# Running the decay levels of both head pairs side by side, and four low parts of weights on GpSimd

## The chip, the cores and the metric

The kernel runs on one core of a Trainium2 chip, in one launch. The metric is the device time in microseconds (us); lower is better. The kernel before takes 292.37 us (median of three runs, 292.06 to 292.63). The engines are named as in the profile: PE (TensorE, matrix products), PEld (its weight loads), DVE (VectorE), ACT (ScalarE), POOL (GpSimd) and SP (SyncE, which issues the DMAs).

## The reference

One decoder layer over 512 tokens of width 1024. The input is normalised, and one projection makes eight groups of 512 columns from it. Four of them feed a gated recurrence of four heads (state 128x128, evaluated chunkwise), four feed block-sparse attention of eight heads (width 64). Both results are gated, joined and projected back.

```python
h = _rms_norm(x, norm_w[l])
proj = jnp.einsum("btd,dc->btc", h, w_in[l])
hq, hf, hi, hg, aq, ak, av, ag = jnp.split(proj, split_points, axis=-1)
o_h = _rms_norm(_hgrn2(hq, hf, hi, lower_bounds[l]), hg_norm_w[l]).reshape(B, T, HG_WIDTH)
o_h = o_h * jax.nn.silu(hg.astype(jnp.float32))
o_a = _moba(aq, ak, av, q_norm_w[l], k_norm_w[l]) * jax.nn.silu(ag.astype(jnp.float32))
x = x + jnp.einsum("btc,cd->btd", jnp.concatenate([o_h, o_a], axis=-1), w_out[l])
```

In the recurrence, with forget gate f, key k = 1 - f and value i, the state follows S_t = diag(f_t) S_{t-1} + k_t i_t^T, and the readout is o_t = S_t^T q_t.

## The kernel before

**Projection.** Operands are split into a high and a low part, and each product is made of three matrix products: high by high, low by high and high by low. Weights arrive in 40 pieces of 256 rows by 512 columns (`load`, lines 90 to 103). `split_hi` casts a piece to its high part `whi` on ACT (line 109); `split_lo` subtracts it to get the low part `wlo` (line 117), on GpSimd if the piece's number is in `POOL_LO`, else on DVE, and then issues the load of the piece three further on. A group takes four pieces, 4g to 4g+3. It is computed in four units of 128 rows; a unit is 24 products of 128x512, in trace and order `acc<-...`. The last unit of a group frees its pieces one by one and splits the piece six further on. Group 1 makes the gate f and the key k, group 2 the recurrence's q, group 3 its output gate G, group 4 the attention's gate gT, groups 5, 6 and 7 the attention's K, Q and v.

**Levels.** The decay inside a chunk of 128 tokens is handled by `levels(pr)` (lines 332 to 446), a generator for one pair of heads. It waits until f, k and q of its pair are there. POOL multiplies neighbouring gates together into products over 2, 4, ... 128 tokens (line 365). Then come five steps. In each PE multiplies blocks of k by blocks of q into a PSUM tile `pl`: 32 products of 32x64 in each of the first three steps, 16 of 32x32 in the fourth, 8 of 64x64 in the fifth. Each product is two instructions in the trace. DVE merges the result (line 351) or ACT copies it into the matrix `AT` (lines 415, 430, 443), and DVE scales q and k by the gate products for the next step (line 357).

**States, chunks, readouts.** When both pairs are through, `states()` turns k (`tp<-ident,k`), copies it to SBUF on ACT (line 458), multiplies it by the values (`us`) and builds the next state S on DVE (lines 466, 471), three times. `chunks()` computes the output of a chunk (`ops`: 4 products for chunk 0, 8 for each later one, since these also read S). `readout()` squares it on ACT (line 496), reduces it on DVE (line 498), raises it to the power -0.5 on POOL (line 163), scales it on DVE (line 505) and turns it on PE (`tp<-ident,scr`); ACT and DVE split the result into `mThh` and `mThl` (lines 516, 517).

**Order.** PE's order is fixed while the program is written, by a planner with a clock of its own. Every generator yields a latency from the table `LAT` and names of things it waits for; `drive` (line 203) steps a generator once its latency has passed on that clock, and fills in projection products (`fill_a`, line 817) as long as none is ready. At one place the filler itself stops. When the first unit of group 5 has been computed, `ev_qk` must reuse the buffers of f and k, and calls `wait_for("chunks")`:

```python
    def wait_for(*keys):
        while not all(kk in done for kk in keys):
            advance()
```

`advance` (line 198) moves the planner's clock to the next ready generator and steps it, with no filler in between. Orders of DVE, ACT and POOL are made by the tile framework; each engine runs its instructions strictly in its order.

Of the kernel before, what the change touches and what calls it, by code (L numbers as in the profile page):

```python
# [21 lines left out]
def kernel(  # L22
# [90 lines left out]
    def split_lo(n):  # L113
        raw = W.pop(("raw", n))
        hi, lo = W[n]
        eng = nc.gpsimd if n in POOL_LO else nc.vector
        eng.tensor_sub(lo, raw, hi.bitcast(F32))  # L117
# [3 lines left out]
    def split(n):  # L121
        if n < len(stream):
            split_hi(n)
            split_lo(n)

    POOL_LO = (3,)
    LAT = dict(lm=4.544, lev0=9.2567, lev=4.4882, copy=1.9908, rms=5.7036, silu=15.1764, qk=14.2881, soft=2.5598, softn=0.0041, acopy=4.5215, st=1.5748, ch=6.6909, DEPTH=2)
    SEQ = 'y10 nt t00 wh0 y1 t01 l00 y2 p00 wl0 p10 l01 t10 q00 t11 q10 l10 wh1 p30 q30 l11 wl1 p20 q20 t03 sq0 t12 t02 sq1 p01 q01 wh2 l03 l12 sq3 wh3 p21 q21 p11 q11 sq2 l02 p31 q31 wl2 p32 q32 rs wl3 p02 q02 p22 q22 cv t13 p12 q12 rr cm l13'
    DSEQ = 'x00 nw x10 w0 x20 x30 x01 x31 x11 w1 x21 w2 w4 v w3 w5'
    POOL_LO = (3,)  # L130
    for w in DSEQ.split():
        if w == "nw":
            nc.sync.dma_start(out=vec[32:40, :], in_=norm_w.rearrange("o (k p) -> (o k) p", p=P))  # L133
# [38 lines left out]
    def mm(o, a, b, start, stop, us):  # L172
        nc.tensor.matmul(o, a, b, start=start, stop=stop)  # L173
        clock[0] += us
# [5 lines left out]
    def spawn(gen, lat=0.0):  # L180
        threads.append([clock[0] + lat, (), gen, lat])
# [88 lines left out]
    def acc_tile(wide):  # L270
        return (psc if wide else pacc).tile([P, 512], F32, tag="sc" if wide else "acc", name="acc")
# [29 lines left out]
    def ev_i(u, ps):  # L301
        nc.scalar.activation(it[:, u, :], ps, AF.Copy, scale=rst[:, u:u + 1])
# [29 lines left out]
    def levels(pr):  # L332
# [4 lines left out]
        kk, qq = k[:, hs, :], q[:, hs, :]  # L337

        def blocks32(qs, w):
            pl = psc.tile([P, 512], F32, tag="sc", name="pl")  # L340
            plv = pl[:, 0:256 * w].rearrange("p (m w c) -> p m w c", w=w, c=32)
            for m in range(8):
                hd, n = divmod(m, 4)
                for b in range(4):
                    t0 = n * P + b * 32
                    mm(plv[b * 32:b * 32 + 32, m], kk[:, hd, t0:t0 + 32], qs[:, :, hd, t0:t0 + 32],
                       True, True, 0.035 if w == 1 else 0.047)
            return plv
# [7 lines left out]
        def mul(o, a, b):  # L356
            nc.vector.tensor_tensor(o, a, b, op=ALU.mult)
# [21 lines left out]
        def up_k(l):  # L379
            v, shape = halves(kk, l)  # L380
            mul(v[:, :, 0, :], v[:, :, 0, :], TB[l][:, :, 1:2].to_broadcast(shape))

        yield LAT["lev0"]
        plv = blocks32(q2[:, :, hs, :], 2)
# [7 lines left out]
        for l in (2, 4):  # L392
# [7 lines left out]
            mul(p0[:, :, 3, :], p0[:, :, 1, :], T4[:, :, 1:2].to_broadcast(one))  # L400
            yield LAT["lm"]
            plv = blocks32(q2[:, :, hs, :], 2)
# [13 lines left out]

        yield LAT["lev"]
        pl = psc.tile([P, 512], F32, tag="sc", name="pl")
        plv = pl[:, 0:128].rearrange("p (m c) -> p m c", c=32)
        atv = at.rearrange("p (m o) t -> p m o t", o=2)  # L420
        for m in range(8):
            hd, n = divmod(m, 4)
# [10 lines left out]

        yield LAT["lev"]
        pl = psc.tile([P, 512], F32, tag="sc", name="pl")
        plv = pl[:, 0:256].rearrange("p (m c) -> p m c", c=64)
        for m in range(8):
            hd, n = divmod(m, 4)
# [5 lines left out]
        up_q(7)  # L444
        up_k(7)
        done[("lev", pr)] = clock[0]

    S = [None] * NT

    def states():  # L450
        yield (LAT["st"], ("lev", 0), ("lev", 1))
        for n in range(NT - 1):
            cs = slice(n * P, (n + 1) * P)
            tp = ptr.tile([P, 512], F32, tag="tr", name="tp")
            for h in range(HH):
                tr(tp[:, h * P:(h + 1) * P], k[:, h, cs])
            kst = scratch()
            nc.scalar.copy(kst, tp)
            yield LAT["copy"]
            us = psc.tile([P, 512], F32, tag="sc", name="us")  # L460
            for h in range(HH):
                es = slice(h * DK, (h + 1) * DK)
                mm(us[:, es], kst[:, h * P:(h + 1) * P], it[:, n, es], True, True, 0.218)
            Sn = scratch()
            if n == 0:
                nc.vector.tensor_copy(Sn, us)
            else:
                for h in range(HH):
                    es = slice(h * DK, (h + 1) * DK)
                    m = (h % 2) * 4 + n  # L470
                    nc.vector.scalar_tensor_tensor(Sn[:, es], S[n][:, es], TL[h // 2][:, m:m + 1], us[:, es],
                                                   op0=ALU.mult, op1=ALU.add)
            S[n + 1] = Sn
            done[("S", n + 1)] = clock[0]

    def chunks():
        yield (LAT["st"], ("lev", 0), ("lev", 1))
        for n in range(NT):
            cs = slice(n * P, (n + 1) * P)
            ops = psc.tile([P, 512], F32, tag="sc", name="ops")  # L480
            for h in range(HH):
                es = slice(h * DK, (h + 1) * DK)
                mm(ops[:, es], AT[h // 2][:, (h % 2) * 4 + n, :], it[:, n, es], True, n == 0, 0.218)
                if n > 0:
                    mm(ops[:, es], q[:, h, cs], S[n][:, es], False, True, 0.218)
            spawn(readout(n, ops), LAT["rms"])
            if n < NT - 1:
                yield (LAT["ch"], ("S", n + 1))
        done["chunks"] = clock[0]
# [97 lines left out]
    DEPTH = LAT.get("DEPTH", 2)  # L587
# [77 lines left out]
    def start_attention():  # L665
        for p in range(NP):
            c_ = {}
            for m, tiles in enumerate(UNITS):
                spawn(attn_unit(p * len(UNITS) + m, p, tiles, c_))
# [147 lines left out]
    def fill_a():  # L817
        const_tri()
        yield from group(1, True, ev_f)
        yield from group(2, True, ev_silu_t(q2[:, 0]))  # L820
        yield from group(3, False, ev_silu(G))
        yield from group(4, True, ev_silu_t(gT))
        const_dist()
        yield from group(5, False, ev_qk("K", ("f", "k", "i", "KL"), kgs))
        yield from group(6, False, ev_qk("Q", ("q",), qgs))
        yield from group(7, False, ev_v)

    with tc.manual_schedule(engines={mybir.EngineType.PE}):
        with tc.manual_schedule():
            accs = {}  # L830

            def part(u, kp, low):
                us = slice(u * P, (u + 1) * P)
                if u not in accs:
                    accs[u] = acc_tile(u >= 2)
                hi, lo = W[kp]
                for d in range(2):
                    kt = 2 * kp + d
                    wh, wl = hi[:, d, :], lo[:, d, :]
                    prods = ((hTh[:, kt, us], wl),) if low else ((hTh[:, kt, us], wh), (hTl[:, kt, us], wh))  # L840
                    for j, (a, b) in enumerate(prods):
                        mm(accs[u], a, b, kt == 0 and not low and j == 0, kt == KT - 1 and low, 0.216)

            def part_hi(u, kp):
                part(u, kp, False)

            def part_lo(u, kp):
                part(u, kp, True)

            acts = dict(cm=const_masks, cv=const_vec, sq=x_sq, rs=x_rstd, rr=x_rows, y=warm_up, nt=nw_col, t=x_turn, l=x_lo, p=part_hi, q=part_lo,  # L850
                        wh=split_hi, wl=split_lo)
            for w in SEQ.split():
                name = w.rstrip("0123456789")
                acts[name](*([int(w[1:])] if name == "y" else [int(ch) for ch in w[len(name):]]))
            for n in range(4, WB):
                split(n)
            for u in range(4):
                part_hi(u, 3)
                part_lo(u, 3)
                ev_i(u, accs[u])  # L860
            for kp in range(4):
                del W[kp]
                split(kp + WB)

        q2 = big.tile([P, 2, HH, T], F32, tag="q", name="q2")
        q = q2[:, 1]
        G = big.tile([P, NT, 512], F32, tag="G", name="G")
        gT = big.tile([P, NP, T], F32, tag="gT", name="gT")
        spawn(levels(0))
        spawn(levels(1))  # L870
        spawn(states())
        spawn(chunks())
        fa = fill_a()
        started = [False]

        def filler():
            yield from fa
            start_attention()
            wait_for(*[("read", n) for n in range(NT)])
            yield from out_h()  # L880

        drive(filler())
        for _ in out_a():
            pass
# [27 lines left out]
```

## Time and profile before

| what | value |
|---|---|
| median of three runs | 292.37 us |
| profiled execution, its own time | 292.67 us |
| its span, first to last instruction | 290.9 us |
| PE busy | 285.0 us (98%) |
| PE weight loads busy | 237.3 us (82%) |
| DVE busy | 174.6 us (60%) |
| ACT busy | 131.5 us (45%) |
| POOL busy | 57.9 us (20%) |
| mean granted TensorE clock | 0.999 |

The profiled execution's own time is 1.8 us longer than its span. Products on PE overlap: one of 128x512 is shown at some 0.39 us, but a new one starts every 0.23 us. So the duration of a row is not what a product adds; the chain of waits, which counts from start to start, shows that. A share of busy time is a mean over stages. In the stretch of the levels DVE is at nearly all of its time, in others below half.

### The profile page before, as it was taken

What the parts mean: (1) busy time and instruction counts of PE and PEld (TensorE: products, weight loads), DVE (VectorE), ACT (ScalarE), POOL (GpSimd) and SP (SyncE); (2) the same over time, 40 slices, a digit from 0 to 9 for tenths busy, and PEclk for the clock granted to TensorE, in tenths of its full rate; (3) what the DMA queues carried; (4) which work ended last, traced back from release to release, by engine and by line L of the source; (5) the groups of instructions that cost most, each with busy time, mean ns of one, the idle gap of its engine ahead of it and who ended that gap; (6) DMA issues with size and microseconds to landing.
All of it is one profiled execution on the core that took longest, in us unless ns stands there. A gap on an engine that the chain in (4) does not pass through costs nothing.

```text
span 290.9 us, 5079 instructions
## 1 busy us (share of the span) xinstructions
PE 285.0 (98%) x1957; PEld 237.3 (82%) x1957; DVE 174.6 (60%) x371; ACT 131.5 (45%) x241; POOL 57.9 (20%) x92
## 2 busy tenths in 40 slices
PE   8899999999999999999999999999999999999995
PEld 8687888888887777898888888888888888888884
DVE  2754654743799998257855685485385577543222
ACT  2674824520520474225511743645676797652000
POOL 1005101082000000010273223420005555320000
PEclk9999999999999999999999999999999999999999
DMA  6964475250350007000620099457269000000132
GB/s 211 357 220 154 16 120 190 89 200 0 97 196 2 2 2 263 28 0 0 218 74 0 2 266 203 109 152 217 49 196 330 0 2 0 2 2 2 72 115 101
DMA packets 21642, 31.00 MB, mean 107 GB/s; under 512 B 1509, under 2 KB 8434, under 8 KB 21618
## 3 DMA queue, kind: packets, MB, share of 16 engines
q1 hardware_dynamic: 21618, 30.68, 35.8%
q8 instruction: 15, 0.25, 0.3%
q14 instruction: 9, 0.07, 0.1%
HBM read 25.17 MB, written 2.10 MB: 94 GB/s over the span
## 4 chain that ended last, share of the span: by engine, by line
PE 95%; DMA 2%; SPq 0%; ACT 0%; POOL 0%; DVE 0%; issue 0%
PE acc L173 76%; PE tp L177 6%; PE sc L173 3%; PE ot L173 3%; PE pl L173 3%; PE ops L173 2%; DMA raw<-in_w_in_dram 2%; PE us L173 1%; ACT whi L109 0%; SPq L71 0%; POOL scr L627 0%; DVE res L733 0%; SPq L133 0%; PE tpv L794 0%; PE rp L232 0%
## 5 line engine op out<-in xcount | busy, mean ns | idle before, releaser
L173 PE MATMUL acc<-whi,hTh 128*128 128x512 f32 x160 | 64.7, 404 | 1.1 <-ACT whi L109 1.1
L173 PE MATMUL acc<-whi,hTl 128*128 128x512 f32 x160 | 62.7, 392 | 0.0
L173 PE MATMUL acc<-wlo,hTh 128*128 128x512 f32 x160 | 60.0, 391 | 0.0
L117 DVE TENSOR_TENSOR wlo<-raw,whi 128x1024 fp32r<-128x1024 f32 x39 | 47.2, 1233 | 9.6 <-ACT whi L109 9.3
L109 ACT CAST whi<-raw 128x1024 fp32r<-128x1024 f32 x40 | 41.6, 1050 | 15.1 <-DMA raw<-in_w_in_dram 7.3
L173 PE MATMUL acc<-hTh,whi 128*128 128x512 f32 x96 | 38.1, 397 | 0.0
L173 PE MATMUL acc<-hTh,wlo 128*128 128x512 f32 x96 | 37.5, 391 | 0.0
L173 PE MATMUL acc<-hTl,whi 128*128 128x512 f32 x96 | 37.4, 389 | 0.0
L163 POOL TENSOR_TENSOR r<-v,mh 128x8 f32<-128x8 f32 (+1 forms) x12 | 17.2, 1430 | 99.5 <-DVE v L161 99.4
L173 PEld LDWEIGHTS acc<-whi,hTh 128*128 128x128 f32 x160 | 30.1, 188 | 7.5 <-ACT whi L109 1.3
L173 PEld LDWEIGHTS acc<-whi,hTl 128*128 128x128 f32 x160 | 30.0, 188 | 6.7 <-DVE hTl L266 0.3
L173 PEld LDWEIGHTS acc<-wlo,hTh 128*128 128x128 f32 x160 | 29.9, 188 | 5.6
L627 POOL TENSOR_SCALAR scr<-scr,rl 128x512 f32<-128x512 f32 (+3 forms) x32 | 17.7, 565 | 39.6 <-DVE rl L625 33.8
L173 PEld LDWEIGHTS acc<-hTh,wlo 128*128 128x128 f32 x96 | 18.0, 188 | 4.0 <-DVE wlo L117 0.2
L173 PEld LDWEIGHTS acc<-hTl,whi 128*128 128x128 f32 x96 | 18.1, 188 | 3.5
L173 PEld LDWEIGHTS acc<-hTh,whi 128*128 128x128 f32 x96 | 18.0, 188 | 3.5
L697 DVE TENSOR_TENSOR res<-acc,res 128x512 f32<-128x512 f32 x15 | 10.3, 689 | 17.1 <-PE acc L173 14.6
L173 PE MATMUL acc<-whi,mTa 128*128 128x512 f32 (+1 forms) x72 | 20.4, 367 | 0.0
L622 ACT ACTIVATE scr<-scr,nm 128x512 f32<-128x512 f32 (+3 forms) x32 | 17.7, 555 | 3.1 <-DVE nm L619 3.0
L177 PE MATMUL tp<-ident,scr 128*128 128x128 f32 x128 | 18.4, 275 | 0.3 <-POOL scr L627 0.3
L177 PEld LDWEIGHTS tp<-ident,scr 128*128 128x128 f32 x128 | 14.8, 140 | 3.6 <-POOL scr L627 0.7
L619 DVE CUSTOM_DVE_ANT_0 scr<-sc,bias 128x512 f32<-128x512 f32 (+3 forms) x32 | 14.1, 484 | 5.5 <-PE sc L173 5.5
(139 smaller groups left out, 427.0 us busy)
## 6 DMA issues: line engine op xcount, KB each, us to landing
raw<-in_w_in_dram SPq DMA_DIRECT2D x32, 512.0 KB, 4.9
raw<-in_w_out_dram SPq DMA_DIRECT2D x8, 512.0 KB, 4.5
x<-in_x_dram SPq DMA_DIRECT2D x8, 256.0 KB, 6.9
res<-in_x_dram SPq DMA_DIRECT2D x8, 256.0 KB, 6.4
out_dram<-res SPq DMA_DIRECT2D x7, 256.0 KB, 2.1
K<-K SPq DMA_DIRECT2D x8, 128.0 KB, 5.7
KL<-KL SPq DMA_DIRECT2D x8, 128.0 KB, 5.8
Q<-scr SPq DMA_DIRECT2D x8, 128.0 KB, 2.7
```

Of the source, the lines that this page charges most:

```text
L109: nc.scalar.copy(hi, raw)
L117: eng.tensor_sub(lo, raw, hi.bitcast(F32))
L163: nc.gpsimd.tensor_tensor(r, v, mh[:, 0:n], op=ALU.pow)
L173: nc.tensor.matmul(o, a, b, start=start, stop=stop)
L177: nc.tensor.transpose(o, a, ident)
L619: nc.vector.tensor_tensor_reduce(out=z[:, o:o + n], in0=sc[:, o:o + n], in1=bias[:, j, T - n:T], op0=ALU.add, op1=ALU.min, scale=1.0, scal ...
L622: nc.scalar.activation(z[:, o:o + n], z[:, o:o + n], AF.Exp, bias=nm[:, e:e + 1], scale=-1.0, accum_out=l[:, e:e + 1])
L627: nc.gpsimd.tensor_scalar(z[:, o:o + n], z[:, o:o + n], rl[:, e:e + 1], 1.0, op0=ALU.mult, op1=ALU.mult)
L697: nc.vector.tensor_tensor(res[hf][:, u, :], ps, res[hf][:, u, :], op=ALU.add)
```

## The change

A new generator `both` steps the two `levels` generators together, and only one thread is spawned where there were two. It multiplies the latencies: the first wait by 1, the second by 1.25, all later ones by 2.3. Four more pieces, 16, 17, 20 and 21, get their low part on GpSimd. The list `POOL_LO` and the table `LAT` change in two entries each; nothing else does.

```diff
-    POOL_LO = (3,)
+    POOL_LO = (3, 16, 17, 20, 21)
...
+    def both(*gens):
+
+        n = 0
+        while True:
+            waits = [next(g, None) for g in gens]
+            if waits[0] is None:
+                return
+            lats = [w if isinstance(w, tuple) else (w,) for w in waits]
+            factor = (1.0, LAT["first"])[n] if n < 2 else LAT["two"]
+            yield (factor * max(w[0] for w in lats), *(kk for w in lats for kk in w[1:]))
+            n += 1
...
-        spawn(levels(0))
-        spawn(levels(1))
+        spawn(both(levels(0), levels(1)))
```

`LAT` gains `two=2.3, first=1.25`. The `pl` blocks of the two pairs now stand next to each other on PE, five pieces instead of nine; between these stand 51, 51, 48 and 6 products of the projection. The first block comes 57 projection products later than before. The last of the 6 is the 24th product of group 5's first unit, which is where `wait_for("chunks")` stands.

PE at the turn from levels to states, the kernel before. `acc` are projection products, here of group 4; `tp<-ident,k`, `ops` and `us` belong to chunk 0 and to the first states.

```order
L177 MATMUL tp<-ident,k 128x128 x4
L173 MATMUL ops<-it,AT_364 128x128 x2
L173 MATMUL ops<-it,AT_366 128x128 x2
L173 MATMUL acc<-hTh,whi 128x512
L173 MATMUL acc<-hTl,whi 128x512
L173 MATMUL acc<-hTh,wlo 128x512
...
L173 MATMUL us<-it,scr 128x128 x4
L177 MATMUL tp<-ident,k 128x128 x4
```

The same place on PE now, from the end of group 5's first unit on (its last three products are the first three rows). The piece goes on in the same way, with no `acc`, through `ops` of chunks 1, 2 and 3 and the turns of readouts 0 and 1, up to the last `ops` of chunk 3.

```order
L173 MATMUL acc<-whi,hTh 128x512
L173 MATMUL acc<-wlo,hTh 128x512
L173 MATMUL acc<-whi,hTl 128x512
L173 MATMUL pl<-q_431,k 64x64 x16
L177 MATMUL tp<-ident,k 128x128 x4
L173 MATMUL ops<-it,AT_364 128x128 x2
L173 MATMUL ops<-it,AT_366 128x128 x2
L173 MATMUL us<-it,scr 128x128 x4
L177 MATMUL tp<-ident,k 128x128 x4
L173 MATMUL us<-it,scr 128x128 x4
L177 MATMUL tp<-ident,k 128x128 x4
L173 MATMUL us<-it,scr 128x128 x4
```

What moved: the projection products that stood between these blocks (6, 12, 12, 3, 24, 15 and 15 of them) now all stand ahead of the fifth step or behind chunk 3. Every block follows directly on the one that it depends on.

DVE around the scaling for the fourth and fifth step, the kernel before. `q<-q,LV 128x16x32` and `k<-k,LV 128x16x32` are the scaling behind the fourth step, `128x8x64` that behind the fifth.

```order
L117 TENSOR_TENSOR wlo<-raw,whi 128x1024 x3
L357 TENSOR_TENSOR q_431<-q_431,LV 128x16x32
L357 TENSOR_TENSOR k<-k,LV 128x16x32
L324 SCALAR_TENSOR_TENSOR G<-acc,rst,scr 128x512
L117 TENSOR_TENSOR wlo<-raw,whi 128x1024
L357 TENSOR_TENSOR q_431<-q_431,LV 128x8x64
L357 TENSOR_TENSOR k<-k,LV 128x8x64
```

The same place now; L799, L801 and L802 build the attention's distance tile.

```order
L117 TENSOR_TENSOR wlo<-raw,whi 128x1024 x2
L314 TENSOR_TENSOR scr<-acc,R 128x512
L117 TENSOR_TENSOR wlo<-raw,whi 128x1024
L317 TENSOR_TENSOR gT<-scr 128x512
L799 CAST scr<-scr 128x512
L357 TENSOR_TENSOR q_431<-q_431,LV 128x16x32
L801 TENSOR_SCALAR scr<-scr 128x512
L357 TENSOR_TENSOR k<-k,LV 128x16x32
L802 TENSOR_TENSOR Dm<-scr 128x512
L357 TENSOR_TENSOR q_431<-q_431,LV 128x16x32
L357 TENSOR_TENSOR k<-k,LV 128x16x32
```

What moved: four scalings stand behind one another where two did, with the evacuation of group 4 and three low parts (pieces 23 to 25) ahead of them, and four more follow for the fifth step.

POOL from the keys k on, now. In the kernel before, the products of neighbouring gates (L365) follow the four `k` directly, and no `wlo` stands here.

```order
L309 TENSOR_SCALAR k<-f 128x512 x4
L117 TENSOR_TENSOR wlo<-raw,whi 128x1024
L365 TENSOR_TENSOR scr<-f 128x512 x2
L365 TENSOR_TENSOR LV<-scr 128x256 x2
L365 TENSOR_TENSOR LV<-LV 128x128 x2
L365 TENSOR_TENSOR LV<-LV 128x64 x2
L365 TENSOR_TENSOR LV<-LV 128x32
L117 TENSOR_TENSOR wlo<-raw,whi 128x1024
```

What moved: the gate products of both pairs stand behind the low part of piece 16, and that of piece 17 stands among them. Those of 20 and 21 follow behind all of them.

## Rows read from the trace of the kernel before

**Rows 1.** The page, part 1: busy us (share of the span) xinstructions, by engine.
```profile
PE 285.0 (98%) x1957; PEld 237.3 (82%) x1957; DVE 174.6 (60%) x371; ACT 131.5 (45%) x241; POOL 57.9 (20%) x92
```
**Rows 2.** Waits of PE: us in total, times, longest us.
```profile
PE acc L173 <- ACT whi L109: 1.1, 1, 1.1
PE tp L177 <- POOL scr L627: 0.3, 1, 0.3
```
**Rows 3.** Chain that ended last, in order of time: start us, us, what; levels.
```profile
78.82 1.03 PE pl L173 x64
79.85 5.66 PE acc L173 x24
...
114.11 0.62 PE pl L173 x16
114.72 2.27 PE acc L173 x9
...
188.82 5.48 PE acc L173 x24
```
**Rows 4.** The same chain, states and chunks.
```profile
116.99 0.44 PE tp L177 x4
...
127.91 1.78 PE ops L173 x16
...
148.07 4.10 PE acc L173 x18
152.16 0.44 PE tp L177 x4
```
**Rows 5.** Stretches: us, then busy us (instructions) by engine, PEclk, DMA share, GB/s.
```profile
90.00:100.00 10.00, 10.00 (x227) 7.66 (x216) 10.00 (x26) 3.33 (x9) 0.00 (x0) 1.00 0.01 3
289.00:290.90 1.90, 0.00 (x0) 0.00 (x0) 0.00 (x0) 0.00 (x0) 0.00 (x0) 0.81 0.09 30
```
**Rows 6.** Timeline of DVE: start us, us, instruction [idle before <-releaser].
```profile
86.68 0.44 DVE L351 COPY_PREDICATED LV<-lmask,pl 128x256 f32<-128x256 int32 x1
...
89.95 0.75 DVE L357 TENSOR_TENSOR q<-q,LV 128x256 f32<-128x256 f32 x2
...
107.33 3.49 DVE L117 TENSOR_TENSOR wlo<-raw,whi 128x1024 fp32r<-128x1024 f32 x3
110.74 0.68 DVE L357 TENSOR_TENSOR q<-q,LV 128x512 f32<-128x512 f32 x1
111.34 0.69 DVE L357 TENSOR_TENSOR k<-k,LV 128x512 f32<-128x512 f32 x1
...
126.35 0.69 DVE L498 TENSOR_REDUCE ss<-scr 128x4 f32<-128x512 f32 x1 [0.48 <-ACT scr L496]
...
128.36 1.12 DVE L505 SCALAR_TENSOR_TENSOR scr<-ops,r,G 128x128 f32<-128x128 f32 x4 [1.12 <-POOL r L163]
...
132.48 0.75 DVE L517 SCALAR_TENSOR_TENSOR mThl<-tp,col,mThh 128x512 fp32r<-128x512 f32 x1
```
**Rows 7.** Timeline of ACT.
```profile
125.23 0.59 ACT L458 COPY scr<-tp 128x512 f32<-128x512 f32 x1 [3.51 <-PE tp L177]
125.71 0.60 ACT L496 ACTIVATE scr<-ops 128x512 f32<-128x512 f32 x1
...
131.76 0.69 ACT L516 ACTIVATE mThh<-tp,col 128x512 fp32r<-128x512 f32 x1 [0.95 <-PE tp L177]
```
**Rows 8.** Timeline of POOL at its one low part of weights.
```profile
26.11 2.39 POOL L117 TENSOR_TENSOR wlo<-raw,whi 128x1024 fp32r<-128x1024 f32 x1
```
**Rows 9.** Timeline of POOL at the gate products.
```profile
59.71 2.01 POOL L365 TENSOR_TENSOR scr<-f 128x512 f32<-128x512 f32 x1
...
64.58 1.04 POOL L365 TENSOR_TENSOR scr<-f 128x512 f32<-128x512 f32 x1
```
**Rows 10.** Timeline of DVE at the same time.
```profile
59.56 1.25 DVE L117 TENSOR_TENSOR wlo<-raw,whi 128x1024 fp32r<-128x1024 f32 x1 [0.52 <-ACT whi L109]
```
**Rows 11.** Timeline of PE at the start of the program.
```profile
1.04 4.64 PE L241 MATMUL wp<-scr 128*128 128x128 f32 x20 [1.04 <-DVE warm L151]
```

More of the change, by code (lines that the diff above doesn't have):

```diff
@@ L124, in split @@
             split_lo(n)
-    POOL_LO = (3,)
-    LAT = dict(lm=4.544, lev0=9.2567, lev=4.4882, copy=1.9908, rms=5.7036, silu=15.1764, qk=14.2881, soft=2.5598, softn=0.0041, acopy=4.5215, st=1.5748, ch=6.6909, DEPTH=2)
+    POOL_LO = (3, 16, 17, 20, 21)
+    LAT = dict(lm=4.544, lev0=9.2567, lev=4.4882, copy=1.9908, rms=5.7036, silu=15.1764, qk=14.2881, soft=2.5598, softn=0.0041, acopy=4.5215, st=1.5748, ch=6.6909, DEPTH=2, two=2.3, first=1.25)
     SEQ = 'y10 nt t00 wh0 y1 t01 l00 y2 p00 wl0 p10 l01 t10 q00 t11 q10 l10 wh1 p30 q30 l11 wl1 p20 q20 t03 sq0 t12 t02 sq1 p01 q01 wh2 l03 l12 sq3 wh3 p21 q21 p11 q11 sq2 l02 p31 q31 wl2 p32 q32 rs wl3 p02 q02 p22 q22 cv t13 p12 q12 rr cm l13'
     DSEQ = 'x00 nw x10 w0 x20 x30 x01 x31 x11 w1 x21 w2 w4 v w3 w5'
-    POOL_LO = (3,)
+    POOL_LO = (3, 16, 17, 20, 21)
     for w in DSEQ.split():
```

## The prediction

> **What bounds the kernel now.** I read the page's busy times first, then the waits of PE, the chain of waits, the stretches, and at the end the timelines of DVE, ACT and POOL around the change. PE is busy for 285.0 of 290.9 us [rows 1]. After its start it waits once for ACT, 1.1 us, and once for POOL, 0.3 us [rows 2]; in the whole stretch of levels and states it waits for nobody. The chain there runs through PE alone, and its pieces give the price of a product: 24 undisturbed projection products add 5.48 us, so 0.228 each [rows 3]. DVE is full in the levels, 10.00 us of 10 [rows 5], but nobody on the chain waits for it. So work on DVE, ACT and POOL is hidden by PE's projection products, and a change can pay only through PE's own pieces. It can cost wherever PE is left without products to put between dependent steps.
>
> **The pieces of the levels: a gain of 0.8 us.** PE's instructions are the same in number; only their order changes. Between the first `pl` block and the last of the nine, and behind that, stand nine pieces of projection products, 123 products in all (the first and the last are in [rows 3]); together they take 29.9 us where 123 times 0.228 is 28.1. So each turn from `pl` to projection costs 0.2 us. Five blocks in place of nine save four such turns, 0.8 us. The bounds are nothing and the whole 1.8 us. The turns among states and chunks cost no more than 0.1 us in all, and I count nothing there.
>
> **The forced run: a loss of 9.0 us.** In the order of the changed kernel the fifth step, the three states and the chunks follow each other with no projection product in between. They did not before: there the 432nd projection product, the last of group 5's first unit, is the third of the 18 at 148.07, behind chunk 3 [rows 4]. Behind these blocks on PE's queue stands everything else, so each wait is added to the time. I follow the run hop by hop, with t = 0 at the end of that 432nd product.
>
> DVE comes first. From the third step's block to the first scaling of q behind the fourth it has 14 merges and scalings at 0.40 us (ten of them ran from 86.68 to 90.70), four low parts at 1.16, four evacuations of group 4 at 0.60 and a cast of 0.4, in all 13.1 us [rows 6]. PE gives it 14.5 us from the end of the first pair's third block to t = 0 (1.0 of the second pair, 48 products, 0.8 of `pl`, six products, two turns). Two of the evacuations also wait for a sigmoid on ACT; with one of these waits, 0.7 us, uncovered, the first scaling starts at t = -0.8. It can't start before -1.9, where its own block ends, and with both waits open and more it starts at 0.5.
>
> DVE then runs ten instructions, one every 0.60 us (110.74 to 111.34), the last of them 0.68 long [rows 6]. The third is done at 1.1, the sixth at 2.9: these release the two fifth-step blocks, 0.62 us each by [rows 3]. The tenth is done at 5.3, which releases the last two turns of k; they are through at 5.55. Chunk 0's `ops` take 0.89 us (half of the 16 at 127.91 [rows 4]; the `us` blocks have its size), to 6.45, and cover the first copy of k. The first `us` goes to 7.35. Then twice: four turns 0.44 [rows 4], 0.28 until ACT's copy starts and PE sees its end, the copy 0.59 [rows 7], `us` 0.89; so 2.2 us each, to 11.75. Chunk 1's `ops` follow, 1.78, to 13.5.
>
> Now PE wants the turns of readout 0. Its square stands behind the third copy on ACT and starts 0.48 after that copy [rows 7], at 10.7; the reduction follows 0.64 later, the scaling 2.01 after that start (126.35 to 128.36, with POOL's power in between), and it lasts 1.12 [rows 6]: done at 14.45, turns through at 14.6, chunk 2 through at 16.4. Readout 1 has its square early, but DVE's queue holds `mThl` of readout 0 ahead of its reduction, and that needs `mThh` from ACT, 0.69 [rows 7], after the turns. `mThl` starts at 15.55 and holds the queue for 0.66, the reduction starts at 16.2, the scaling at 18.2, done at 19.35; the turns are through at 19.5 and chunk 3 at 21.3. PE's own work in this run is 1.24 of `pl`, five times 0.44 of turns, 0.89, three times 0.89 and three times 1.78, in all 12.3 us. The rest, 9.0 us, is waiting, and the longest single wait is the 2.7 us ahead of readout 1's turns. Bounds: 7.1 if DVE has caught up (-1.1) and half of the 14 hops are covered (-0.7); 10.7 if DVE is late (+1.3) and waking PE costs 0.05 us more at each of eight waits.
>
> What hid these steps before were the 87 projection products that stood between them. They are not lost but come later, when nothing needs covering: at 152.16, where readout 2's turns stand [rows 4], both kernels have done the same PE work, and the order from there on differs by three products. The wait for readout 2's turns is covered by 15 products; nothing later has less slack than before.
>
> **The low parts on GpSimd: a loss of 0.5 us.** They take four times 1.16 us from DVE, worth nothing on PE where PE did not wait. One on POOL takes 2.39 us [rows 8]. Pieces 16 and 17 stand ahead of and among the gate products, which are now needed some 10 us after; 16, 17, 20 and 21 are themselves used a group later, over 20 us. But piece 21 is done just when DVE begins the merges of the second step, two batches of 4.0 us. Behind these on DVE stands the evacuation that frees the buffer of group 4's third unit, and PE gets there 33 products and one `pl` half, 8.8 us, after the batch can start; 8.0 plus 0.69 leaves no slack. The trace has one row on a meeting of the two engines: a gate product of 512 columns took 2.01 us on POOL [rows 9] while DVE subtracted a low part [rows 10], and 1.04 with DVE idle. So one of two waits. Between nothing and 2.4 us I take 0.5, nearer to nothing, since the two overlap at most in part.
>
> The Trainium skill speaks against the move: its page "SBUF — State Buffer", section "SBUF: two separate sides", says that VectorE with two SBUF inputs and GpSimd share a pair of ports under an exclusive lock held for a whole instruction. The two rows agree with it, with POOL as the loser. By that rule the full 2.4 us is lost if POOL comes first, and nothing if DVE does.
>
> **The sum.** 9.0 - 0.8 + 0.5 = 8.7 us. The profiled execution took 292.67 us, its span of 290.9 and 1.8 around it, which is 0.30 above the median of the runs shown. 292.37 + 8.7 gives 301.0 us.
>
> **Rivals.** *The clock falls in the forced run.* For it: in the last 1.9 us, where PE has no instruction at all, the granted clock is 0.81 as a mean, so part of it lies at the lower level of 1.2 GHz [rows 5]; and at the start of the program 20 products of 128x128 took 4.64 us, 0.23 each [rows 11] against 0.11 in [rows 4], half speed. Against it: in this run PE works between the waits, and no wait in the middle of the program is long enough to show a fall. If it falls in the 2.7 us wait and stays down for 4.6 us as at the start, half of that is added: 303.3 us. The Trainium skill's page "TensorE: Matmul & The Clock Gate", section "Why this matters for your kernels", warns of such idle gaps between bursts; by that the clock falls here only if 2.7 us is too long.
>
> *GpSimd's low parts hold DVE up.* If DVE loses at each meeting, the second step's batch is 2.4 us late and PE stands at group 4's third unit: 1.9 more than I took, 302.9 us. For it the missing slack, against it the row above, where POOL lost.
>
> *Not slower.* The ends of PE's products are modelled, and DVE is at 10.00 of 10 us: PE may have waited for DVE in the levels without the view of waits telling it. Then the longer spacing gives back the whole 1.8 us, and if DVE, relieved of four low parts, runs far ahead, the forced run shrinks. It decides at waits of 1.8 us in that run. Against it: the three copies and two readouts alone leave 5.1 us of waits that no faster DVE queue removes. Its best would be 290.6 us, and 292.4 where it breaks even.
>
> That the longer spacing is not kept in the end (the last latency is cut off, since `wait_for` steps on without products) is no rival but the cause of the forecast.
>
> **How the numbers follow.** Forecast 0.75, clock 0.12, DVE held up 0.09, not slower 0.04. The bounds of the terms add up to 5.3 and 13.1 us, 297.7 to 305.5; eight in ten should lie in 298.0 to 304.8, which takes in both rivals on the slower side. About 0.2% is what a measurement of this kernel can tell from no change. The last rival splits into 0.02 faster, 0.01 the same and 0.01 slower, so slower by over 0.2% has 0.97.
>
> **What would show it.** The waits of PE should show some 9 us in about eight waits between 133 and 157 us, by DVE (k, readout scalings) and ACT (copies), the longest ahead of readout 1's turns; the 51 products between `pl` blocks should run with one turn of 0.2 us per piece; an idle time at group 4's third unit would be the low parts. The granted clock should stay at 1.00 there. The prediction is wrong if PE's waits there stay below 5 us, or if the time after 157 us differs from before.

## The result, and the profile after

The changed kernel takes 305.13 us (median of six executions, 302.94 to 305.77) where the kernel before took 292.5 us beside it: a ratio of 1.0438, with a 95% interval of 1.0414 to 1.0463, so 12.6 us slower (12.1 to 13.5 by the ratio). The forecast was 301.0 us with a range up to 304.8. The direction and the place were right; the size was 4 us short. Now and then an execution of any kernel is disturbed and some per cent longer at a lower clock; the ratios leave those out, and the trace of "The pairing alone" below is of one.

The profiled execution took 302.94 us, the shortest of the six. Its busy times, part 1 of the page, answer to [rows 1]: PE is busy 2.8 us longer and its share falls from 98% to 96%.

```profile
PE 287.8 (96%) x1957; PEld 239.1 (79%) x1957; DVE 171.8 (57%) x367; ACT 131.2 (44%) x241; POOL 67.1 (22%) x96
```

The waits of PE (us in total, times, longest) answer to [rows 2], where only two short ones stood besides the one at the start:

```profile
PE pl L173 <- DVE k L357: 3.1, 2, 1.9
PE tp L177 <- DVE scr L517: 2.1, 1, 2.1
PE us L173 <- ACT scr L470: 1.5, 2, 0.7
...
PE tp L177 <- DVE k L357: 0.7, 1, 0.7
PE acc L173 <- DVE scr L314: 0.4, 1, 0.4
```

The first four are hops of the forced run, the longest sum first: six waits and 7.4 us, where some 9 us in about eight were expected. The last is group 4's third unit. Here is PE's timeline in the run (start us, us, instruction, [idle before <- releaser]); the first row is the 432nd projection product, the last the first one after the run:

```profile
133.50 0.40 PE L173 MATMUL acc<-whi,hTl 128*128 128x512 f32 x1
135.84 0.69 PE L173 MATMUL pl<-q,k 128*64 128x64 f32 x16 [1.93 <-DVE k L357]
137.64 1.12 PE L173 MATMUL pl<-q,k 128*64 128x64 f32 x16 [1.12 <-DVE k L357]
...
140.63 1.92 PE L173 MATMUL ops<-it,AT 128*128 128x128 f32 x8
142.34 1.91 PE L173 MATMUL us<-it,scr 128*128 128x128 f32 x8
144.04 0.64 PE L177 MATMUL tp<-ident,k 128*128 128x128 f32 x4
145.42 1.16 PE L173 MATMUL us<-it,scr 128*128 128x128 f32 x8 [0.73 <-ACT scr L470]
...
155.69 1.01 PE L177 MATMUL tp<-ident,scr 128*128 128x128 f32 x4 [2.14 <-DVE scr L517]
...
158.24 0.48 PE L173 MATMUL acc<-whi,hTh 128*128 128x512 f32 x1
```

Two things are to be seen. Every wait stands between small blocks, and nothing else is on PE's queue. And the second `pl` block takes 1.12 us where the first took 0.69, and eight `us` products 1.91 where eight more take 1.16 three microseconds later. That is the clock, as the stretches show (us, then busy us of PE, PEld, DVE, ACT and POOL, PEclk, DMA share, GB/s; a PEclk of 0.50 is 1.2 GHz, 1.00 is 2.4 GHz); [rows 5] had 1.00 in the levels:

```profile
136.00:138.00 2.00, 0.88 (x23) 0.77 (x22) 2.00 (x4) 0.74 (x2) 0.00 (x0) 0.82 0.21 80
138.00:140.00 2.00, 1.44 (x17) 0.87 (x14) 1.90 (x4) 0.74 (x2) 0.00 (x0) 0.50 0.00 0
142.00:144.00 2.00, 2.00 (x11) 2.00 (x11) 0.00 (x0) 0.00 (x0) 0.00 (x0) 0.50 0.00 0
144.00:146.00 2.00, 1.27 (x11) 1.03 (x10) 0.69 (x1) 0.59 (x1) 0.00 (x0) 0.97 0.00 0
```

PE goes down to 1.2 GHz from about 137.3 to 144.1 us, 6.8 us long, after two waits with one short block between them. It does not go down at the 2.14 us wait.

The first block starts 1.0 us later than forecast because DVE came late. The chain of waits (start us, us, what) answers to [rows 6]; there DVE went from one instruction to the next, here it waits for a load:

```profile
126.25 1.15 DVE wlo L117
127.42 3.39 DMA raw<-in_w_in_dram
...
130.91 1.06 ACT whi L109
...
131.99 1.23 DVE wlo L117
133.21 0.60 DVE gT L317
133.81 0.34 DVE scr L799
134.15 0.60 DVE q L357
```

The low part of piece 22 on DVE frees the buffer of piece 25, whose load is issued only then. Its high part on ACT and its low part on DVE follow, and this low part stands in DVE's queue ahead of the last level's first scaling.

With t = 0 at 133.73 us (the 432nd product's start and 0.23), the hops of the forecast against the trace:

| step done | forecast t | measured t | late by |
|---|---|---|---|
| DVE's first scaling starts | -0.8 | 0.34 | 1.1 |
| first `pl` block starts | 1.1 | 2.11 | 1.0 |
| turns of k through | 5.55 | 6.90 | 1.35 |
| first `us` through | 7.35 | 10.31 | 3.0 |
| third `us` through | 11.75 | 15.01 | 3.3 |
| readout 1's turns through | 19.5 | 22.80 | 3.3 |
| run over | 21.3 | 24.51 | 3.2 |

About 1.0 us comes from DVE at the head, about 2.2 from the clock while it is low (the run with the clock held up, below, gives the same 2.2), and nothing after that: copies, readouts and POOL's power took what [rows 6, 7] gave. PE's own work in the run is 12.3 us, so 12.2 are lost in it instead of 9.0.

### The profile page after: what moved, and what is told of

The parts are those of the page before. It is cut to its first block, busy times and chain, and to the rows that moved or that the text cites. A ratio compares the mean times of both kernels' runs of the same rounds, so it can differ in the third digit from the quotient of the medians.

```text
span 301.1 us, 5074 instructions
## 1 busy us (share of the span) xinstructions
PE 287.8 (96%) x1957; PEld 239.1 (79%) x1957; DVE 171.8 (57%) x367; ACT 131.2 (44%) x241; POOL 67.1 (22%) x96
## 4 chain that ended last, share of the span: by engine, by line
PE 83%; DVE 9%; DMA 4%; ACT 2%; issue 1%; POOL 1%; SPq 0%; ACTq 0%; DVEq 0%; POOLq 0%
PE acc L173 65%; PE tp L177 7%; PE ot L173 3%; PE sc L173 3%; DVE q L357 3%; DVE k L357 2%; DMA res<-in_x_dram 2%; PE ops L173 2%; PE pl L173 2%; PE us L173 1%; DMA x<-in_x_dram 1%; DMA raw<-in_w_in_dram 1%; DVE LV L351 1%; DVE wlo L117 1%; ACT whi L109 1%
## 5 line engine op out<-in xcount | busy, mean ns | idle before, releaser
L173 PE MATMUL acc<-whi,hTh 128*128 128x512 f32 x160 | 64.0, 400 | 0.8 <-ACT whi L109 0.8
L109 ACT CAST whi<-raw 128x1024 fp32r<-128x1024 f32 x40 | 41.5, 1051 | 19.7 <-DMA raw<-in_w_in_dram 12.1
L117 DVE TENSOR_TENSOR wlo<-raw,whi 128x1024 fp32r<-128x1024 f32 x35 | 42.4, 1229 | 10.1 <-ACT whi L109 9.7
L177 PE MATMUL tp<-ident,scr 128*128 128x128 f32 x128 | 19.7, 280 | 2.4 <-DVE scr L517 2.1
L117 POOL TENSOR_TENSOR wlo<-raw,whi 128x1024 fp32r<-128x1024 f32 x5 | 12.0, 2393 | 31.0 <-ACT whi L109 31.0
```

The lines of the kernel that those rows point to most:

```text
L109: nc.scalar.copy(hi, raw)
L177: nc.tensor.transpose(o, a, ident)
```

## The experiments

A ratio is against the kernel before in the same set of runs; "+6.4 us" is what such a ratio has above 1, times 292.5.

**The low parts alone.** The kernel before, with this edit only:

```
-    POOL_LO = (3,)
+    POOL_LO = (3, 16, 17, 20, 21)
```

> The kernel before with the four low parts 16, 17, 20, 21 on GpSimd and nothing else. Theory (the cut of the run of products by the wait for the chunks is the loss): no cut here, so within 0.5 us of the kernel before, 291.9 to 293.0, with a wait of about 0.4 us at group 4's third unit. Rival (GpSimd's low parts of 2.4 us each hold VectorE or the weights up): 294.5 or more, with waits of the products on wlo.

Ratio 1.0032 (1.0011 to 1.0054): +0.9 us (0.3 to 1.6). That is more than the 0.5 us the theory allowed, and less than half of what the rival asked for. The wait that the theory expected at group 4's third unit is not there; PE waits for DVE's scalings twice among the levels instead:

```profile
PE pl L173 <- DVE k L357: 0.6, 1, 0.6
PE pl L173 <- DVE q L357: 0.4, 1, 0.4
```

**The pairing alone.** The changed kernel with `POOL_LO = (3,)`.

> The changed kernel with the four low parts back on VectorE. Theory (taking both pairs together is the loss): 303 to 307, as the changed kernel or a little later, since VectorE has 4 x 1.2 us more to do before the last scaling; the same eight waits between the last level and the fourth chunk. Rival (the low parts on GpSimd are the loss): 292 to 295.

Ratio 1.0430 (1.0401 to 1.0458), 305.49 us: as the changed kernel. Giving the four low parts back to VectorE recovers nothing, so they are not the loss. Only its times are used here.

**TensorE kept busy.** The changed kernel with

```
+    def keep(tile, n):
+        for _ in range(n):
+            nc.tensor.matmul(tile[:, 256:512], hTh[:, 0, 0:P], hTh[:, 0, 0:256], start=True, stop=True)
```

called ahead of the two `pl` blocks (14, 11), the last two turns of the first k (6), the second and third `us` (6 each) and readouts 0 and 1 (8, 16).

> The changed kernel with 67 products of 128x256 that nothing reads, put into free halves of PSUM tiles ahead of the blocks that wait, so that TensorE stays busy through the waits. It takes out the lower clock and leaves every wait for another engine. Theory (the lower clock costs 2 to 4 us of the 12.6 and the waits the rest): granted clock 0.997 or more, ops and us blocks back at 1.06 us for eight, 301.5 to 303.5. Rival 1 (the clock's fall is hidden by the waits): clock 1.00 but 304.5 to 306. Rival 2 (the clock is most of the loss): under 300.

Ratio 1.0325 (1.0293 to 1.0357), 302.08 us, granted clock 0.993 to 1.000 in its four executions: 3.3 us less than the changed kernel by the ratios. The stretches of the run:

```profile
136.00:140.00 4.00, 3.43 (x49) 2.88 (x48) 4.00 (x8) 1.20 (x4) 0.00 (x0) 1.00 0.25 92
140.00:144.00 4.00, 3.94 (x35) 3.71 (x34) 1.51 (x3) 1.12 (x3) 0.00 (x0) 1.00 0.00 0
```

PEclk is 1.00 where it was 0.50. From the 432nd product's start to the end of the run PE needs 22.5 us in place of 24.7. The theory holds: the clock is about 3 us of the median, and the 9.5 us that this kernel still loses are the waits, less what the other terms give back.

**Kept busy in the first two waits only** (14 and 11 products, the other calls left out).

> The changed kernel with the unused products of e4 in the two waits of the last level only (14 and 11 of them); the later waits of 0.7, 0.7, 0.7 and 2.1 us are left empty. Theory (the clock falls for the two waits of 1.93 and 1.12 us with a short block between, and for no later one): granted clock 0.997 or more, 301.5 to 303.2, like e4. Rival 1 (the 2.1 us wait ahead of readout 1's turns, the one that the prediction named, drops the clock too): a stretch at 0.50 after 150 us, 303.3 to 305. Rival 2 (the unused products only delay): 305 or more.

Ratio 1.0377 (1.0345 to 1.0409), 303.27 us: rival 1, in the profiled execution and, by their mean clock of 0.994, in two more of the five. The other two, 302.69 and 302.98 us, have 1.000 and 0.998, no fall that the mean would show. Filling the first two waits moves the fall in most executions, and avoids it in some. The stretches of the profiled execution around the fourth chunk:

```profile
154.00:156.00 2.00, 1.31 (x6) 1.04 (x7) 1.77 (x6) 0.11 (x1) 0.16 (x1) 0.85 0.00 0
156.00:158.00 2.00, 2.00 (x12) 2.00 (x11) 0.88 (x3) 1.16 (x2) 1.71 (x3) 0.50 0.00 0
158.00:160.00 2.00, 2.00 (x11) 1.82 (x11) 1.79 (x6) 0.00 (x0) 1.44 (x3) 0.80 0.00 0
```

Now the clock falls at the 2.14 us wait, the one that the forecast's rival named, and stays low into the projection products. In the changed kernel's own traces it had already fallen and come back before that wait, and held. That is no rule either: in two kernels below (more low parts, earlier load) it had also fallen and come back, and fell at that wait again. One and the same wait went both ways, and what decides it stays open.

**The long spacing without the pairing.** The kernel before, its pairs as two threads, with the four low parts on GpSimd and the spacings

```
-    LAT = dict(lm=4.544, lev0=9.2567, lev=4.4882, ...
+    LAT = dict(lm=10.4512, lev0=11.5709, lev=10.3229, ...
```

> The kernel before, its pairs one by one, with GpSimd's four low parts and with the spacings of the levels as long as in the changed kernel (10.5, 11.6 and 10.3 us in place of 4.5, 9.3 and 4.5). Theory (spacing is the loss, not that both pairs go in one step): from the second pair's last level on no products stand beside the chain, and the waits for it, the states, and readouts 0 and 1 remain: 5 to 8 us, 297 to 302. Rival (pairing is the loss): 292 to 294.

Ratio 1.0218 (1.0165 to 1.0271), 299.08 us. Long spacing without the pairing loses 6.4 us (4.8 to 7.9), of which the low parts, by the first experiment, may be 0.9. Those ahead of the last blocks are gone, since the first pair's now has products behind it; the other waits stand at the same places:

```profile
PE tp L177 <- DVE scr L505: 2.1, 1, 2.1
PE us L173 <- ACT scr L458: 1.5, 2, 0.7
PE tp L177 <- DVE k L357: 1.1, 1, 1.1
```

From the last product ahead of the run to its end pass 18.8 us where the changed kernel has 24.7, and the clock stays at 0.994 or above, although the 2.14 us wait is there too. So the length of the chain is about half of the loss, and the pairing adds the rest. What of it is the eight scalings of both pairs at one time, with two waits for them, and what the clock that falls there, is argued from the traces and not measured one by one.

**The pairing with short spacing.** The changed kernel with `two=1.25` in place of 2.3:

> The changed kernel with the factor of the later spacings 1.25 in place of 2.3, so that both pairs still go together but 27 products stand between two levels in place of 51. Theory (the length of the chain decides, not the pairing): only the end of the chain, readout 1 and the fourth chunk, is still without products, so one wait of 2 to 3 us there; levels wait for VectorE by up to 1 us each, since a step of both pairs took VectorE about 8 us and the spacing is now about 8.2; 295 to 298. Rival (pairing by itself costs, through VectorE): 300 or more, with waits of the level blocks on q or k.

Ratio 1.0247 (1.0203 to 1.0291), 300.02 us. The forced run is nearly gone (one wait of 0.4 us at readout 1, even less than the 2 to 3 us of the theory), but the level blocks wait 4.7 us for q, as the rival had it, and the clock falls there too, for 6.8 us:

```profile
114.00:116.00 2.00, 2.00 (x50) 1.73 (x43) 2.00 (x6) 0.34 (x1) 0.00 (x0) 0.50 0.03 8
```

DVE's timeline says why, and the row of POOL beside it:

```profile
103.15 0.42 DVE L357 TENSOR_TENSOR q<-q,LV 128x256 f32<-128x256 f32 x1
103.49 2.90 DVE L357 TENSOR_TENSOR k<-k,LV 128x512 f32<-128x512 f32 x1
106.31 2.92 DVE L357 TENSOR_TENSOR q<-q,LV 128x256 f32<-128x256 f32 x2
```

```profile
103.27 5.34 POOL L117 TENSOR_TENSOR wlo<-raw,whi 128x1024 fp32r<-128x1024 f32 x2 [14.52 <-DVE k L357]
```

Two low parts run on POOL for 5.34 us, and in that time DVE is taken up by three scalings that last 1.45 us in the kernel that follows.

**The same with the low parts on VectorE.** `two=1.25` and `POOL_LO = (3,)`:

> The kernel with spacing factor 1.25 (t125_short_spacing) and its four low parts 16, 17, 20, 21 back on VectorE. There the two low parts on GpSimd from 100.7 us on stood beside scalings of 2.90 and 2.92 us (two of 0.41) on VectorE, which take 0.69 and 0.75 elsewhere, and the level blocks behind them waited 4.7 us. Theory (a product or scaling of two operands in SBUF does not run on VectorE while GpSimd does its own; pairing with short spacing is short of VectorE's time on top): every scaling of 128x512 at 0.7 us, waits of the level blocks under 3 us, 295 to 298.5. Rival 1 (the low parts cost VectorE 4.9 us that it does not have there, as much as the holds): 299 to 302. Rival 2 (pairing costs nothing once the spacing is short): 291.5 to 293.5.

Ratio 1.0087 (1.0050 to 1.0123), 295.22 us, 4.7 us under the kernel above. DVE's timeline at the same place:

```profile
103.20 0.42 DVE L357 TENSOR_TENSOR q<-q,LV 128x256 f32<-128x256 f32 x1
103.53 0.69 DVE L357 TENSOR_TENSOR k<-k,LV 128x512 f32<-128x512 f32 x1
104.14 0.76 DVE L357 TENSOR_TENSOR q<-q,LV 128x256 f32<-128x256 f32 x2
```

The holds are gone, the waits of the level blocks come to 1.5 us (1.1 and 0.4), and the clock is at 0.993 or above: the 4.7 us are the holds and the fall of the clock behind them together. So the pairing with neither the long spacing nor the low parts on GpSimd is 2.5 us slower than the kernel before. No kernel of these runs beats it.

**More low parts on GpSimd.** The changed kernel with `POOL_LO = (3, 16, 17, 20, 21, 22, 24, 25)`:

> The changed kernel with three more low parts (22, 24, 25) on GpSimd. Theory (VectorE comes late to the last level because piece 25's load waits for piece 22's low part in VectorE's queue, and the products of the first wait start 1.1 us late for it): first wait of the last level 0.5 to 1.2 us in place of 1.9, 303 to 304.5 where the changed kernel has 305.1, more if the clock then stays up (301 to 303). Rival (GpSimd is itself late with piece 25, 2.4 us for each low part): 305 or more, with a wait of products on wlo.

Ratio 1.0485 (1.0434 to 1.0535), 306.57 us: the rival's time, for a reason that is neither's. The first wait did not shrink, it became one of 4.0 us, and not on the weights but on k. DVE's timeline ahead of the last level, and POOL's:

```profile
125.18 0.69 DVE L357 TENSOR_TENSOR k<-k,LV 128x512 f32<-128x512 f32 x1
...
126.38 2.31 DVE L357 TENSOR_TENSOR k<-k,LV 128x512 f32<-128x512 f32 x1
...
129.75 2.88 DVE L317 TENSOR_TENSOR gT<-scr 128x512 f32<-128x512 f32 x1
...
133.15 2.53 DVE L799 CAST scr<-scr 128x512 f32<-128x512 int32 x1
```

```profile
125.26 2.88 POOL L117 TENSOR_TENSOR wlo<-raw,whi 128x1024 fp32r<-128x1024 f32 x1 [18.39 <-ACT whi L109]
129.36 2.72 POOL L117 TENSOR_TENSOR wlo<-raw,whi 128x1024 fp32r<-128x1024 f32 x1 [1.22 <-ACT whi L109]
...
133.02 2.39 POOL L117 TENSOR_TENSOR wlo<-raw,whi 128x1024 fp32r<-128x1024 f32 x1 [0.43 <-ACT whi L109]
```

Three low parts on POOL, three instructions on DVE that take 2.3 to 2.9 us in place of 0.4 to 0.7. The first of them, in turn, came 0.08 us after a scaling on DVE (125.18) and took 2.88 us in place of 2.39. The clock falls twice in this trace, from 138.7 to 145.5 us and, behind the wait of 2.15 us at readout 1, from 159.2 to 162.6. I had written the test as one of the load of piece 25 and had not seen this.

**An earlier load.** `RB = 4` in place of 3 and `bufs=8` in place of 10 for the scratch tiles:

> The changed kernel with four buffers for the loads of weights in place of three, so that piece 25's load does not wait for piece 22's low part (eight scratch tiles in place of ten make the room). Theory (VectorE's scalings of the last level come 1.1 us late in the changed kernel because of that load): the first scaling of the last level starts 0.5 to 1.2 us earlier against the end of the run of products, the first wait falls from 1.9 to about 1, 303 to 304.6, or 301 to 303 if the clock then stays at 2.4 GHz. Rival (the load is no cause; VectorE's own queue sets it): 304.7 to 306, first wait unchanged at 1.8 to 2.0.

Ratio 1.0445 (1.0404 to 1.0486), 305.80 us: the rival's time with the theory's mechanism. The first scaling did start earlier (1.6 us ahead of t = 0, where it was 0.3 behind), and the first wait fell from 1.93 to 0.89 us. But the load's place in DVE's queue was taken by the evacuation behind it (`gT`, 0.69 us, and the cast), the second wait rose from 1.12 to 1.46, and the two together fell only from 3.1 to 2.3. The clock still fell, now for 3.4 us, and once more at readout 1's wait, where products of one kind go from 0.39 to 0.64 us:

```profile
136.41 0.69 PE L173 MATMUL pl<-q,k 128*64 128x64 f32 x16 [0.89 <-DVE k L357]
138.56 0.69 PE L173 MATMUL pl<-q,k 128*64 128x64 f32 x16 [1.46 <-DVE k L357]
...
155.80 1.01 PE L177 MATMUL tp<-ident,scr 128*128 128x128 f32 x4 [2.14 <-DVE scr L517]
...
157.71 0.64 PE L173 MATMUL ops<-it,AT 128*128 128x128 f32 x2
```

The run is 0.6 us shorter (24.15), but PE waits longer elsewhere: 1.6 us for its first weights in place of 0.8, and 1.0 for POOL late in the span in place of 0.2. The fewer scratch tiles may be the reason, which no run separates. That the load is the last releaser is shown; that removing it gives back the 1.0 us at the head is not.

**Products left beside the chain.** The wait for the chunks is taken out of the evacuation of keys and queries, and their turns wait instead:

```
     def qk_tr(key, u, nrm, gain, tags):
-        yield LAT["qk"]
+        yield (LAT["qk"], "chunks")
...
-            if u == 0:
-                wait_for("chunks")
```

> The changed kernel with the wait for the chunks taken out of the evacuation of keys and queries; only their turns wait for the chunks, 3.0 us apart, and the projection's products go on between levels, states, chunks and readouts. Both pairs still go together, the low parts stay on GpSimd. Theory (the loss is the stretch in which nothing but the chain of small blocks is left for TensorE): clock 1.00, waits of TensorE between the last level and the fourth chunk under 2 us in all, 291 to 293. Rival 1 (both pairs in one step are slow by themselves, through VectorE): 295 to 300 with waits before the level blocks. Rival 2 (the loss is only put off, to the turns of keys and queries or the tail): 294 to 298 with the wait after 170 us.

Ratio 1.0739 (1.0714 to 1.0764), 314.94 us. The waits from the last level to the fourth chunk are gone (0.2 us left), and the time is worse by 9 us than the changed kernel's. It is rival 2, larger than I priced it:

```profile
PE acc L173 <- DVE res L713: 6.3, 1, 6.3
PE sc L173 <- DMA Q<-scr: 4.5, 2, 4.2
```

Chunk 3 ends at 178.7 us here, at 147.8 in the kernel before. The products that covered the chain had been the cover of what follows, and the attention stands without any, with the clock at 0.50 from 220 to 236 us and from 240 to 246. Two more kernels bring the turns closer, so that the scores come after as many products as before:

> As e5 (no wait for the chunks at the evacuation of keys and queries), but the eight turns of keys and queries come 1.0 us after the fourth chunk and 1.5 us apart, where e5 left 14.3 and 3.0 us, so that scores start after as many products as in the kernel before. Theory (e5's loss was its late turns, with no products left beside the attention; the chain's length is not lost as long as other products stand beside it): no wait of TensorE over 1 us between 130 and 250 us, clock 1.00, 291 to 293.5. Rival (the chain is now too long for the stock of products wherever the waits stand): 296 or more, with waits before the scores.

> As e5b, with 2.5 us between the turns of keys and queries in place of 1.5; the scores start after the same count of products. In e5b TensorE waited 9.1 us for the turn tiles, which VectorE's low parts of K freed late. Theory (the long chain itself costs nothing where products stand beside it, only the crowding of the turns did): waits of the turns under 2 us, clock 0.995 or more, 292 to 296. Rival (after a chain this long VectorE and ScalarE have too much to do before the scores at any spacing): 299 or more, with waits of the turns or scores on VectorE or on a DMA.

With 1.5 us between turns the ratio is 1.0513 (1.0459 to 1.0567), with 2.5 us 1.0330 (1.0296 to 1.0363). In both the clock falls again, and the rival holds: the turns wait for the low parts of K on DVE, 9.1 us in three waits and, in the second,

```profile
PE tp L177 <- DVE KL L564: 6.9, 2, 3.6
```

So the loss is not only the one wait that cuts the spacing off. In these four kernels the longer chain was paid for either way: 12.6 us with the forced run, 9.7, 15.0 and 21.6 us with the waits in front of the scores. The cheapest of them is 3.2 us under the changed kernel by the ratios, so some of the loss went with the move, most of it did not.

**The changed kernel itself, twice more.**

> The changed kernel itself, once more. Its profiled execution took 302.94 us where the median of six is 305.13; its clock was at 0.50 for 6.8 us, once. Theory (the slower executions are the same but for the clock: it falls a second time at the wait ahead of readout 1's turns, or stays low longer): at 304.5 to 306 the same waits within 0.5 us in all, and 10 us or more at 0.50. Rival (the slower executions wait longer for VectorE or a DMA): waits of TensorE 2 us longer in all at the same length of the low clock.

> The same as after_again1: at 304.5 to 306, theory 10 us or more at 0.50 and the same waits, rival 2 us more of waits. At 302.5 to 303.5, both expect about 7 us at 0.50.

304.32 and 304.39 us, both with a granted clock of 0.989. Both have the same waits as the first (7.6 and 7.7 us in the run, 7.4 there), one fall of the same length, and no second. The run took 25.1 us where it took 24.7; in the first execution the first product also started earlier (7.91 us, against 8.25 and 8.57, and 9.13 in the kernel before). So neither theory holds for these two: 304.3 is one fall of the clock. For the executions at 305.0 to 305.8 no trace exists. Three of them have a mean clock of 0.982 or 0.983; I estimate from it 10 to 11 us at 0.50 in place of 6.8, and the kernel with more low parts, at 0.983, shows 10.2 us in two falls. So a second fall fits them but is not shown, and the one at 305.29 us with a clock of 0.988 stays open.

## Why the prediction was short

*The bound.* Right. PE bounds the kernel before, and the change was paid where PE had no products beside the chain. After the run hardly anything more is lost: readout 2's turns stand at 161.9 us, 9.8 later than in [rows 4], and the span ends 10.2 later. The 9.8 are the 12.2 us of the run, 0.4 at group 4's third unit, 1.5 gained at the turns, and 1.2 because this execution's first product started earlier (7.91 us against 9.13), which no term had; so the profiled execution is the shortest of six.

*The forced run, 9.0 us.* The step that failed is its head and its clock, which the sum put at nothing, and not its hops. The head was worked out with DVE free from its queue, the first scaling at -0.8 and the worst case at 0.5; it was 0.34, because piece 25's load and its high part stood in DVE's way. I had counted DVE's instructions and two waits for a sigmoid, and not that a low part is itself the end of a chain through a DMA. That is 1.0 us. From the turns of k to the end, the hops came out as forecast once the clock is taken off: with TensorE kept busy the run takes 22.3 us from t = 0 (22.5 less 0.23), against a forecast of 21.3, and the head is the difference.

*The clock.* It was a rival of 0.12, placed at the wait ahead of readout 1, for 2.3 us. It falls in every profiled execution of the changed kernel, and costs 2.2 us in the run and about 3 in the median. That the rival's price was near is luck, since it belonged to another wait. I argued that no wait was long enough, from single waits; the trace has it fall after 1.93 and 1.12 us with 0.69 us of small products between. The Trainium skill's page "TensorE: Matmul & The Clock Gate", section "Why this matters for your kernels", warns of idle gaps between bursts. The trace agrees that gaps take the clock down (PEclk 0.50 between 138 and 144 us), but here each was shorter than the gap that the page warns of. Forecast plus head plus clock (301.0 + 1.0 + 2.2) is 304.2, near the two later executions at 304.3 and 304.4; that is in part luck, as the turns were 0.7 too small and the first product started 0.9 and 0.6 us earlier there than in the kernel before.

*The turns between blocks, -0.8 us.* Too small. From the first `pl` block at 90.45 us to t = 0 PE takes 43.3 us. The products are 156 times 0.228, so 35.6, the blocks 7.0 and the wait at group 4's third unit 0.4. That leaves 0.3 us for the turns of four pieces where nine had 1.8 before, a gain of some 1.5. So a turn in the changed kernel cost less than the 0.2 us at which it was priced.

*The low parts, +0.5 us.* Right in size and place: 0.4 us at group 4's third unit (0.7 and 0.4 in the later two). The mechanism behind it I had half right. In the changed kernel DVE has little to do beside the low parts: two instructions are held, by 0.5 us (at 78.36) and 0.3. The second is in the batch of the second step, beside the low part of piece 21 (103.69 to 106.07), near where the prediction had it; the same kind of instruction takes 0.42 us elsewhere:

```profile
105.68 0.69 DVE L357 TENSOR_TENSOR q<-q,scr 128x256 f32<-128x256 f32 x1
```

Where a low part meets a DVE at work that starts later, DVE is held until POOL's instruction ends, as the rival said: 2.3 to 2.9 us for an instruction. The row in which POOL lost [rows 9] told who came first and not who loses: DVE's low part there started at 59.56, POOL's product at 59.71 [rows 10]. The Trainium skill's "SBUF — State Buffer", section "SBUF: two separate sides", says that whichever of the two starts first keeps the ports for its whole instruction. The traces agree both ways, with POOL first (2.31 us at 126.38 for 0.69) and with DVE first (POOL's 2.88 at 125.26 for 2.39) in the kernel with more low parts.

*Not slower, 0.04.* It was rightly low: the waits for the copies (1.5 us) and for readout 1 (2.1 us) stand in all three traces of the changed kernel, and in the kernel with the long spacing without the pairing.

## What to carry to other kernels

Before spacing a chain of dependent steps wider, count the independent work that will still be there at its end: it was a fixed stock in all four kernels tried here, and what covered a longer chain early was missing later. Price a stretch in which the tensor engine meets several short waits at the lower clock as well; the length of a single wait did not tell it here, as 2.14 us went both ways. Work moved to GpSimd was free here only while VectorE was idle or worked from PSUM, so check what runs beside it in the order, not the busy shares.

## What was not expected of the hardware

- The clock fell after waits of 1.93 and 1.12 us with a block of 0.69 us between, and it held through one wait of 2.14 us in the same execution. With the first two waits filled, it fell at that 2.14 us wait, and in two further kernels it fell at both places.
- A subtraction of 128x1024 on GpSimd (2.39 us alone) held VectorE's products of two SBUF operands until its own end (0.69 us became 2.31 to 2.90) and also an integer cast with one operand (0.42 became 2.53). An evacuation with an operand in PSUM (L314) took its usual 0.69 us at 76.96 in the changed kernel, inside a low part that ran from 76.56 to 78.96.
- GpSimd pays as well when VectorE comes first: one of its low parts took 2.88 us in place of 2.39, having started 0.08 us after a product of 0.69 us on VectorE (125.26 and 125.18, with eight low parts on GpSimd).
